# A two-block transformer on one core: the first norm ahead of the state-space set-up, four gate tiles in the state-space stage

## The chip, the cores and the metric
The kernel runs on one core of one Trainium2 chip. The metric is the device time of one execution in microseconds (us). The engines are PE (TensorE, matmul), DVE (VectorE), ACT (ScalarE), POOL (GpSimd) and SP (SyncE, which issues most DMAs). Each engine takes its instructions from one queue, in order.

## The reference, cut to what matters
The change lies in the first quarter of the program, the token mixer. What follows it (a channel mixer, then attention, cross attention and an MLP) is the same in both kernels.

```
h = rmsnorm(x, g_pre)                      # x: 528 tokens x 1024 (16 meta tokens ahead of 512)
u, q, k, v, o, gi, gf, ga, gb = split(h @ w_in)
y_a = gelu(s5_ssm(u, lam, b, c, d, log_dt)) # state space, 32 groups of 16 inputs, 64 states
y_a = y_a * sigmoid(y_a @ w_glu)
hb  = mlstm_chunkwise(conv_silu(q), conv_silu(k), v, gi, gf)   # 4 heads of 128
y_b = rmsnorm_per_head(hb) * sigmoid(o)
merged = sigmoid(ga) * (y_a @ w_a) + sigmoid(gb) * (y_b @ w_b)
x + rmsnorm(merged @ w_out, g_post)
...
def rmsnorm(x, g):
    return x * lax.rsqrt(mean(x * x) + 1e-6) * g
```

## The kernel before
Activations lie as 128 features by tokens. A float32 product is made of three passes of a rounded type: the operands are split into a high and a low part, and PE runs high x high, high x low and low x high. Of a weight tile of 128 output columns, 1024 x 128 numbers come in one DMA (`wst`); ACT rounds them to `whi` (line 125) and DVE, in the mLSTM stage POOL for a part of them, subtracts to get `wlo` (line 126). `product` then gives pieces: for each token range of 264 (or 258 and 256) columns, 24 matmuls in three pieces (lines 165, 167, 168), and an eviction behind the last. Eviction of the w_in products multiplies by `rs`, the reciprocal root of the first norm, so no w_in product can leave its PSUM bank before that norm is known. Banks are of two kinds, `mm` and `mx`, taken in turn.

The norm: `next_input` makes the accumulators `nacc`; `add_square` has ACT square each x tile and adds the squares (the first of each accumulator's chain on POOL, the rest on DVE, line 241). `rstd_wide` sums over the partitions with matmuls by a tile of ones (line 257, bank `rs`), ACT takes Ln and Exp (lines 258, 259), and DVE takes one Newton step in four operations (lines 261 to 264). It runs once for each half of the tokens.

The set-up of the state space (`ssm_setup`) is a generator: powers of the complex decay rates by repeated multiplication on DVE (lines 360 to 365, four products, a difference and a sum each), scaled copies of them (404 to 433), and eight products on POOL (395 to 397). It is written behind the norm. `ssm_tile` computes the state space for one of four feature tiles: a set-up product `pp` (451 to 453), transposing matmuls (`tr`, 461 and 485), DVE rotations and scans (519 to 533, the last of them is `xx`), matmuls on `xx` (539), and a gelu (550 to 553) into `ya`. `weave` lays product pieces between these steps: q, k, v and o of the mLSTM (`raw`, eviction in line 719). In the mLSTM stage the fill is the 16 gate tiles (`gate`, eviction in line 791, tanh in 792), and behind them the products of w_glu, which need `ya` and the ring tiles that the heads' o gates leave.

The order of each engine's queue is not that of the source. The framework is opened with `schedule_with_timeline_sim=True` and sorts the instructions of each engine by a plan of its own; `keep_in_program_order` and `issue_after` bind single instructions. Which instruction stands where is therefore read from the built kernels, how long it takes from the trace.

Of the kernel before, what the change touches and what calls it, by code (L numbers as in the profile page):

```python
# [11 lines left out]
FT = mybir.dt.float32  # L12
FR = mybir.dt.float32r
# [6 lines left out]
P = 128  # L20
# [43 lines left out]
class Net:  # L64
# [184 lines left out]
    def rstd_wide(self, out, accs, t, width=DM):  # L249


        nc = self.nc
        V = nc.vector
        n = out.shape[-1]
        ps = self.pmm.tile([P, 512], FT, name="rs", bufs=1)[:, 0:n]
        for j, acc in enumerate(accs):
            nc.tensor.matmul(ps, self.ones, acc, start=j == 0, stop=j == len(accs) - 1)
        nc.scalar.activation(out, ps, AF.Ln, scale=1.0 / width, bias=self.eps)
        nc.scalar.activation(out, out, AF.Exp, scale=-0.5)
        t = t[:, 0:n]  # L260
        V.tensor_tensor(t, out, out, OP.mult)
        V.scalar_tensor_tensor(t, ps, EPS * width, t, OP.add, OP.mult)
        V.tensor_scalar(t, t, -0.5 / width, 1.5, OP.mult, OP.add)
        V.tensor_tensor(out, out, t, OP.mult)
# [32 lines left out]
    def ssm_setup(self, pool, tmp):  # L297
# [106 lines left out]
        V.tensor_scalar(self.al, pr, pos, None, OP.mult)  # L404
        V.tensor_scalar(self.be, pi, -1.0, None, OP.mult)
        for j in range(TC):
            V.tensor_copy(self.qr[:, j, :], pr[:, TC - 1 - j, :])
            V.tensor_scalar(self.qi[:, j, :], pi[:, TC - 1 - j, :], neg, None, OP.mult)
# [21 lines left out]
        V.tensor_copy(hir[:, 8, :], er[9])  # L430
        V.tensor_copy(hii[:, 8, :], ei[9])
        V.tensor_scalar(loi, loi, pos, None, OP.mult)
        V.tensor_scalar(hii, hii, pos, None, OP.mult)
# [270 lines left out]
    def mixer(self):  # L704
# [3 lines left out]
        with ExitStack() as es:  # L708
# [5 lines left out]
            yas = [self.yab.tile([P, L], FT, name=f"ya{f}") for f in range(4)]  # L714
            raws = {}

            def raw(i, h):
                t = raws[i, h] = self.ring.tile([P, L], FT, name=f"r{4 * h + i}")
                return self.product(I["w_in"][4 + 4 * i + h], FULL, lambda ps, t0, n: V.tensor_tensor(
                    t[:, t0:t0 + n], ps, self.rs[:, t0:t0 + n], OP.mult))  # L720

            with ExitStack() as e2:
# [4 lines left out]
                with tc.tile_pool(name="tmp0", bufs=1, side="right", reuse_waits="tile") as tmp:  # L727
                    self.next_input(extra=tmp, more=1)
# [32 lines left out]
                    for (t0, n) in FULL:  # L761
                        self.rstd_wide(rs[:, t0:t0 + n], [a[:, t0:t0 + n] for a in self.nacc],
                                       tmp.tile([P, 264], FT, name="rw"))
# [3 lines left out]
                    for _ in setup:  # L767
                        pass
                self.ssmp = self.pool(e2, "ssmp", 2)
                self.ssmt = self.pool(e2, "ssmt")  # L770
                load, fill = self.chain([self.gate_rows(mx)] + [raw(i, h) for h in range(4) for i in range(4)])
# [7 lines left out]
                self.weave([(steps, fill[first:])])  # L779
                self.pmx = None  # L780
            sgp = self.pool(es, "sgp")
            mt = self.pool(es, "mtmp", 2)
            sga = [sgp.tile([P, LQ], FT, name=f"sga{f}") for f in range(KT)]
            ybs = [self.yab.tile([P, L], FT, name=f"yb{h}") for h in range(4)]
            gb = {}

            def gate(f, out):

                def ev(ps, t0, n):
                    o = out()[:, t0 - T0:t0 - T0 + n]  # L790
                    V.tensor_tensor(o, ps, rs[:, t0:t0 + n], OP.mult)
                    nc.scalar.activation(o, o, AF.Tanh, scale=0.5)
                return self.product(I["w_in"][f], TAIL, ev)
# [6 lines left out]
            with ExitStack() as e2:  # L800
# [10 lines left out]
                gates = [gate(20 + f, lambda f=f: sga[f]) for f in range(KT)] + [  # L811
# [46 lines left out]
            jobs = self.merge(self.pool(es, "memp"), mt, yas, ybs, sga, gb, sgp, a2, b2)  # L858
# [36 lines left out]
    def merge(self, mem, mt, yas, ybs, sga, gb, sgp, a2, b2):  # L895
# [32 lines left out]
        yo = [sgp.tile([P, LQ], FT, name=f"sga{f}") for f in range(KT)]  # L928
# [154 lines left out]
    def bias_rows(self, mt):  # L1083


        nc = self.nc
        self.ed = self.dram.tile([12, P, 640], FT, name="ed")
        self.gd = self.dram.tile([12, 640], FT, name="gd")
        rel = mt.tile([32, 12], FT, name="rel", bufs=1)
        nc.sync.dma_start(rel, self.I["rel"])  # L1090
        for i in range(2):
            c = slice(320 * i, 320 * i + 320)
            oh, am, g = (self.yab.tile([P, L], FT, name=f"{n}{i + j}")[0:m, 0:320]
                         for n, j, m in (("ya", 0, 32), ("ya", 2, 12), ("yb", 0, 12)))
# [440 lines left out]
    def memory_input(self, mp):  # L1535
# [395 lines left out]
```

## Time and profile before

| | |
|---|---|
| time, median of 3 runs | 1567.07 us (1562.07 to 1567.22) |
| profiled execution: own time | 1567.67 us |
| profiled execution: span, first to last instruction | 1564.4 us |
| mean granted TensorE clock | 0.981 of full speed |
| busy PE, DVE, ACT, POOL | 95%, 66%, 46%, 21% |

The profile is of one execution, 3.3 us of which lie outside its span. Its own time stands 0.6 us above the median, so a sum made against it can be compared with the median as it is. The shares are means over stages of different kinds; the first 350 us, which the change touches, are read on their own below.

### The profile page before, as it was taken

What the parts mean: (1) busy time and instruction counts of PE and PEld (TensorE: products, weight loads), DVE (VectorE), ACT (ScalarE), POOL (GpSimd) and SP (SyncE); (2) the same over time, 40 slices, a digit from 0 to 9 for tenths busy, and PEclk for the clock granted to TensorE, in tenths of its full rate; (3) what the DMA queues carried; (4) which work ended last, traced back from release to release, by engine and by line L of the source; (5) the groups of instructions that cost most, each with busy time, mean ns of one, the idle gap of its engine ahead of it and who ended that gap; (6) DMA issues with size and microseconds to landing.
All of it is one profiled execution on the core that took longest, in us unless ns stands there. A gap on an engine that the chain in (4) does not pass through costs nothing.

```text
span 1564.4 us, 25002 instructions
## 1 busy us (share of the span) xinstructions
PE 1479.6 (95%) x9761; PEld 1334.2 (85%) x9761; DVE 1032.0 (66%) x1968; ACT 724.1 (46%) x1400; POOL 335.5 (21%) x308
## 2 busy tenths in 40 slices
PE   5998999999989999999999999999789999999997
PEld 4988999988989899999999877877778888888886
DVE  8887879777577655555475878888887443344334
ACT  5233356664554433334455466575666431134332
POOL 4066721003342000000131445303342000000001
PEclk9998999999999999999999999999999999999998
DMA  5333232227444322223656222113220322333221
GB/s 189 96 98 105 80 120 75 64 74 234 148 136 135 95 93 93 90 95 118 187 152 217 78 67 68 55 44 125 90 81 32 93 95 93 96 94 96 93 94 54
DMA packets 66430, 161.95 MB, mean 104 GB/s; under 512 B 15100, under 2 KB 24556, under 8 KB 66184
## 3 DMA queue, kind: packets, MB, share of 16 engines
q1 hardware_dynamic: 64936, 157.74, 32.3%
q8 instruction: 76, 1.25, 0.3%
q0 software_dynamic: 288, 1.57, 0.3%
q10 hardware_dynamic: 1088, 1.05, 0.2%
q14 instruction: 42, 0.34, 0.1%
HBM read 153.92 MB, written 10.33 MB: 105 GB/s over the span
## 4 chain that ended last, share of the span: by engine, by line
PE 54%; DVE 10%; ACT 3%; issue 1%; DMA 1%; POOL 0%; DVEq 0%; ACTq 0%; POOLq 0%
PE mm L135 6%; PE mm L138 5%; PE mm L136 5%; PE mm L165 5%; PE mm L168 5%; PE mm L167 5%; PE mx L165 4%; PE mx L168 4%; PE mx L167 4%; DVE xl L110 2%; PE mx L135 2%; PE mx L138 2%; PE mx L136 2%; DVE ptl L107 1%; PE tr L1208 1%
## 5 line engine op out<-in xcount | busy, mean ns | idle before, releaser
L126 DVE TENSOR_TENSOR wlo<-wst,whi 128x1024 fp32r<-128x1024 f32 (+2 forms) x227 | 285.0, 1257 | 196.9 <-ACT whi L125 121.2
L125 ACT ACTIVATE whi<-wst 128x1024 fp32r<-128x1024 f32 (+3 forms) x244 | 251.9, 1034 | 302.9 <-PE mm L136 107.3
L168 PE MATMUL mm<-xl,whi 128*128 128x256 f32 (+4 forms) x808 | 233.5, 314 | 0.3 <-DVE xl L110 0.3
L167 PE MATMUL mm<-xh,whi 128*128 128x256 f32 (+4 forms) x808 | 233.1, 314 | 0.2 <-DVE x L1641 0.2
L167 PE MATMUL mx<-xh,whi 128*128 128x512 f32 (+4 forms) x552 | 170.6, 330 | 7.8 <-ACT xh L109 7.7
L168 PE MATMUL mx<-xl,whi 128*128 128x512 f32 (+4 forms) x552 | 170.9, 330 | 3.3 <-DVE xl L110 3.2
L167 PEld LDWEIGHTS mm<-xh,whi 128*128 128x128 f32 (+1 forms) x808 | 153.8, 190 | 9.9 <-DVE x L1670 0.3
L168 PEld LDWEIGHTS mm<-xl,whi 128*128 128x128 f32 (+1 forms) x808 | 153.3, 190 | 10.3 <-issue 0.6
L165 PE MATMUL mm<-xh,wlo 128*128 128x256 f32 (+4 forms) x808 | 139.2, 311 | 0.0
L135 PE MATMUL mm<-hh,whi 128*128 128x256 f32 (+1 forms) x496 | 139.2, 310 | 0.0
L136 PE MATMUL mm<-hl,whi 128*128 128x256 f32 (+1 forms) x496 | 139.0, 310 | 0.0
L165 PEld LDWEIGHTS mm<-xh,wlo 128*128 128x128 f32 (+1 forms) x808 | 116.4, 187 | 9.8 <-issue 0.5
L167 PEld LDWEIGHTS mx<-xh,whi 128*128 128x128 f32 (+1 forms) x552 | 105.8, 192 | 17.1 <-ACT xh L109 8.0
L168 PEld LDWEIGHTS mx<-xl,whi 128*128 128x128 f32 (+1 forms) x552 | 105.6, 191 | 14.3 <-DVE xl L110 4.9
L165 PE MATMUL mx<-xh,wlo 128*128 128x512 f32 (+4 forms) x552 | 104.6, 331 | 0.0
L126 POOL TENSOR_TENSOR wlo<-wst,whi 128x1024 fp32r<-128x1024 f32 (+1 forms) x34 | 75.2, 2217 | 120.5 <-PE mm L138 38.2
L993 POOL TENSOR_TENSOR acc<-acc,osq 128x256 f32<-128x256 f32 (+1 forms) x26 | 25.2, 969 | 344.6 <-ACT osq L990 344.6
L135 PEld LDWEIGHTS mm<-hh,whi 128*128 128x128 f32 x496 | 93.4, 188 | 6.1
L136 PEld LDWEIGHTS mm<-hl,whi 128*128 128x128 f32 x496 | 93.5, 189 | 5.8
L165 PEld LDWEIGHTS mx<-xh,wlo 128*128 128x128 f32 (+1 forms) x552 | 85.5, 193 | 9.4 <-issue 0.2
L138 PE MATMUL mm<-hh,wlo 128*128 128x256 f32 (+1 forms) x496 | 83.6, 310 | 1.9 <-DVE wlo L126 1.9
L138 PEld LDWEIGHTS mm<-hh,wlo 128*128 128x128 f32 x496 | 70.5, 188 | 8.0 <-DVE wlo L126 2.3
(553 smaller groups left out, 3353.3 us busy)
## 6 DMA issues: line engine op xcount, KB each, us to landing
wst<-in_w_in_dram SPq DMA_DIRECT2D x52, 512.0 KB, 3.6
wst<-in_w_down_dram SPq DMA_DIRECT2D x32, 512.0 KB, 3.5
wst<-in_w_mup_dram SPq DMA_DIRECT2D x32, 512.0 KB, 3.5
wst<-in_w_mdown_dram SPq DMA_DIRECT2D x32, 512.0 KB, 3.7
wst<-in_w_gate_dram SPq DMA_DIRECT2D x22, 512.0 KB, 3.5
wst<-in_w_up_dram SPq DMA_DIRECT2D x22, 512.0 KB, 3.6
wst<-in_w_out_dram SPq DMA_DIRECT2D x20, 512.0 KB, 3.6
wst<-in_w_down_dram SPq DMA_DIRECT2D x16, 384.0 KB, 3.5
```

Of the source, the lines that this page charges most:

```text
L107: nc.vector.tensor_tensor(lo, src, hi.bitcast(FT), OP.subtract)
L110: nc.vector.scalar_tensor_tensor(lo, src, gain, hi.bitcast(FT), OP.mult, OP.subtract)
L125: nc.scalar.activation(hi[:, 0:n], st[:, 0:n], AF.Copy)
L126: self.wlow.tensor_tensor(lo[:, 0:n], st[:, 0:n], hi[:, 0:n].bitcast(FT), OP.subtract)
L135: nc.tensor.matmul(ps, ah, bh, start=start and i == 0, stop=False)
L136: nc.tensor.matmul(ps, ah, bl, start=False, stop=False)
L138: nc.tensor.matmul(ps, al, bh, start=False, stop=stop and i == n - 1)
L165: nc.tensor.matmul(ps, wl[:, k], xh, start=False, stop=k == KT - 1)
L167: nc.tensor.matmul(ps, wh[:, k], xh, start=k == 0, stop=False)
L168: nc.tensor.matmul(ps, wh[:, k], xl, start=False, stop=False)
L993: nc.gpsimd.tensor_tensor(acc, acc, sq, OP.add)
L1208: nc.tensor.matmul(yp[0:64, c0:c1], m[:, j, vc:vc + 64], d[:, j - f0, c0:c1], start=ji == x == 0, stop=ji == len(jobs) - 1 and x == 2)
```

## The change
The first norm uses four accumulators in place of two, so that POOL adds two squares and not six, and four ones-matmuls for each half of the tokens and not two. Its banks come from the pool `ptr` and its small tile is one for each half. The rest of the set-up is issued behind the norm's last DVE operation. Twenty scaled copies of the set-up go from DVE to ACT. Four of the sixteen gate tiles (w_in 20 to 23) become fill of the state-space stage, whose list of steps gets eight more empty ones; their output tiles and the mLSTM's `yb` tiles get pools of their own.

```diff
-    def rstd_wide(self, out, accs, t, width=DM):
+    def rstd_wide(self, out, accs, t, width=DM, bank=None):
-        ps = self.pmm.tile([P, 512], FT, name="rs", bufs=1)[:, 0:n]
+        ps = (self.pmm.tile([P, 512], FT, name="rs", bufs=1) if bank is None else bank)[:, 0:n]
         for j, acc in enumerate(accs):
-            nc.tensor.matmul(ps, self.ones, acc, start=j == 0, stop=j == len(accs) - 1)
+            mm = nc.tensor.matmul(ps, self.ones, acc, start=j == 0, stop=j == len(accs) - 1)
+            if bank is not None and j == 0:
+                self.tc.keep_in_program_order(mm)
...
-        V.tensor_tensor(out, out, t, OP.mult)
+        return V.tensor_tensor(out, out, t, OP.mult)
...
-        V.tensor_scalar(self.al, pr, pos, None, OP.mult)
-        V.tensor_scalar(self.be, pi, -1.0, None, OP.mult)
+        copy = lambda to, t, scale=1.0: nc.scalar.activation(to, t, AF.Copy, scale=scale)
+        copy(self.al, pr, pos)
+        copy(self.be, pi, -1.0)
         for j in range(TC):
-            V.tensor_copy(self.qr[:, j, :], pr[:, TC - 1 - j, :])
-            V.tensor_scalar(self.qi[:, j, :], pi[:, TC - 1 - j, :], neg, None, OP.mult)
+            copy(self.qr[:, j, :], pr[:, TC - 1 - j, :])
+            copy(self.qi[:, j, :], pi[:, TC - 1 - j, :], neg)
...
+            sgs = [self.pool(es, "sgp")] * 4
+            sga = [sgs[0].tile([P, LQ], FT, name=f"sga{f}") for f in range(4)]
...
-                    self.next_input(extra=tmp, more=1)
+                    self.next_input(extra=tmp, more=3)
...
-                        self.rstd_wide(rs[:, t0:t0 + n], [a[:, t0:t0 + n] for a in self.nacc],
-                                       tmp.tile([P, 264], FT, name="rw"))
+                        known = self.rstd_wide(rs[:, t0:t0 + n], [a[:, t0:t0 + n] for a in self.nacc],
+                                               tmp.tile([P, 264], FT, name=f"rw{t0}"),
+                                               bank=self.ptr.tile([P, 512], FT, name="tr"))
...
-                    for _ in setup:
-                        pass
+                    with tc.issue_after(known.ins):
+                        for _ in setup:
+                            pass
...
-                load, fill = self.chain([self.gate_rows(mx)] + [raw(i, h) for h in range(4) for i in range(4)])
+                load, fill = self.chain([self.gate_rows(mx)] + [raw(i, h) for h in range(4) for i in range(4)] + [
+                    gate(20 + f, lambda f=f: sga[f]) for f in range(4)])
...
-                self.weave([(steps, fill[first:])])
+                self.weave([(steps + [None] * 8, fill[first:])])
...
-                gates = [gate(20 + f, lambda f=f: sga[f]) for f in range(KT)] + [
+                gates = [gate(20 + f, lambda f=f: sga[f]) for f in range(4, KT)] + [
                     gate(28 + f, lambda f=f: gate_b(f)) for f in range(KT)]
```

From the start of the merge on, the order of every engine's instructions is the same in both kernels. Three places ahead of it:

DVE at the norm. Before, the four steps of the first half (rw, rw, rw, rs) stand among set-up operations (al, be, qi, cm, sm):

```order
L261 TENSOR_TENSOR rw<-rs 128x264
L405 TENSOR_SCALAR be<-pi 128x288
L408 TENSOR_SCALAR qi<-pi,sg 128x32 x3
L360 TENSOR_TENSOR cm_523<-sm_181 128x32
L262 SCALAR_TENSOR_TENSOR rw<-rs,rw 128x264
L361 TENSOR_TENSOR cm_524<-sm_180 128x32
L263 TENSOR_SCALAR rw<-rw 128x264
L362 TENSOR_TENSOR sm_599<-cm_523,cm_524 128x32
L264 TENSOR_TENSOR rs<-rs,rw 128x264
```

In the changed kernel the two halves stand together, and the first set-up operation behind them is the memset of `zero`:

```order
L263 TENSOR_TENSOR rw_359<-rs 128x264
L264 SCALAR_TENSOR_TENSOR rw_359<-tr,rw_359 128x264
L265 TENSOR_SCALAR rw_359<-rw_359 128x264
L266 TENSOR_TENSOR rs<-rs,rw_359 128x264
L263 TENSOR_TENSOR rw_371<-rs 128x264
L751 TENSOR_TENSOR u<-mx,rs 128x33x8 x2
L264 SCALAR_TENSOR_TENSOR rw_371<-tr,rw_371 128x264
L126 TENSOR_TENSOR wlo<-wst,whi 128x64
L265 TENSOR_SCALAR rw_371<-rw_371 128x264
L266 TENSOR_TENSOR rs<-rs,rw_371 128x264
L346 MEMSET zero 16x128
```

The set-up's decay powers are all behind the norm now, and the first evictions of u (line 738 before, 751 now) stand between the norm's halves.

DVE in state-space tile 1, around the `xx` of its first half. Before, the gelu of tile 0, its steps on u and ya (lines 550, 551, 553), stands ahead of it:

```order
L550 TENSOR_SCALAR u<-u 128x528
L466 TENSOR_TENSOR ks<-ks,dd 16x4x16
L551 TENSOR_TENSOR u<-u,yv 128x528
L719 TENSOR_TENSOR r_741<-mx,rs 128x264
L530 TENSOR_TENSOR r<-r,ec 128x264
L531 TENSOR_TENSOR rs<-rs,es 128x264
L553 SCALAR_TENSOR_TENSOR ya_106<-u,yv 128x8x66
L533 TENSOR_TENSOR xx<-r,rs 128x4x65
```

In the changed kernel (lines 553, 554, 556, and 536 for `xx`) they stand behind it:

```order
L536 TENSOR_TENSOR xx<-r,rs 128x4x65
L553 TENSOR_SCALAR u<-u 128x528
L724 TENSOR_TENSOR r_746<-mx,rs 128x264
L554 TENSOR_TENSOR u<-u,yv 128x528
L556 SCALAR_TENSOR_TENSOR ya_106<-u,yv 128x8x66
L469 TENSOR_TENSOR ks<-ks,dd 16x4x16
```

The matmul that waits for `xx` has three DVE operations fewer ahead of it.

PE in the mLSTM stage, second half of head 2 (`st` scores, `num` and `den` their products with v and with ones). Before, products of gate tiles (L167, L168, into mm) stand between:

```order
L168 MATMUL mm<-xl_133,whi 128x258
L135 MATMUL st<-qh,kh 128x256
L136 MATMUL st<-ql,kh 128x256
L138 MATMUL st<-qh,kl 128x256
L167 MATMUL mm<-xh_126,whi 128x258
L168 MATMUL mm<-xl_134,whi 128x258
L135 MATMUL st<-qh,kh 128x128
L136 MATMUL st<-ql,kh 128x128
L138 MATMUL st<-qh,kl 128x128
```

In the changed kernel the gates are used up at this place:

```order
L138 MATMUL num<-sh,vl 128x256
L686 MATMUL den<-sl,ones_85 2x256
L135 MATMUL st<-qh,kh 128x256
L136 MATMUL st<-ql,kh 128x256
L138 MATMUL st<-qh,kl 128x256
L135 MATMUL st<-qh,kh 128x128
L136 MATMUL st<-ql,kh 128x128
L138 MATMUL st<-qh,kl 128x128
L135 MATMUL num<-sh,vh 128x256
L685 MATMUL den<-sh,ones_85 2x256
```

For 40 rows there is nothing between the head's own matmuls. w_glu's products come behind them.

## Rows read from the trace of the kernel before

**Rows 1.** The page, part 1: engine, busy us, share of the span, instructions.
```profile
PE 1479.6 (95%) x9761; PEld 1334.2 (85%) x9761; DVE 1032.0 (66%) x1968; ACT 724.1 (46%) x1400; POOL 335.5 (21%) x308
```

**Rows 2.** Waits of PE from 0 to 400 us: total, times, longest.
```profile
PE rs L257 <- DVE cm L361: 8.9, 1, 8.9
...
PE tr L539 <- DVE xx L533: 5.9, 3, 4.0
PE tr L461 <- DVE pp L453: 2.7, 1, 2.7
...
PE tr L601 <- DVE r L588: 1.1, 1, 1.1
PE st L695 <- ACT sqn L689: 1.0, 1, 1.0
```

**Rows 3.** PE by time around the norm: start, us, engine, line, operation, tiles, idle before.
```profile
27.19 0.71 PE L257 MATMUL rs<-nacc,ones 128*128 128x264 f32 x2 [1.72 <-DVE nacc L241]
...
37.92 2.10 PE L257 MATMUL rs<-nacc,ones 128*128 128x264 f32 x4 [8.93 <-DVE cm L361]
39.48 0.75 PE L167 MATMUL mx<-xh,whi 128*128 128x264 f32 x1
```

**Rows 4.** ACT by time, from the last square to the root.
```profile
27.17 0.42 ACT L240 ACTIVATE sq<-x 128x264 f32<-128x264 f32 x1 [3.24 <-DVE nacc L241]
27.61 1.28 ACT L199 ACT_TABLE_LOAD   x1
...
29.42 0.42 ACT L259 ACTIVATE rs<-rs 128x264 f32<-128x264 f32 x1
```

**Rows 5.** DVE by time, set-up and norm beside each other.
```profile
27.33 0.23 DVE L389 TENSOR_SCALAR sm<-sm,sg 128x32 f32<-128x32 f32 x1
...
30.70 1.38 DVE L408 TENSOR_SCALAR qi<-pi,sg 128x32 f32<-128x32 f32 x2
...
35.41 0.42 DVE L261 TENSOR_TENSOR rw<-rs 128x264 f32<-128x264 f32 x1
...
38.69 1.12 DVE L738 TENSOR_TENSOR u<-mx,rs 128x264 f32<-128x264 f32 x2
```

**Rows 6.** POOL by time: one of the eight set-up products.
```profile
33.27 1.32 POOL L397 TENSOR_TENSOR bb<-bb,tb 128x512 f32<-128x512 f32 x1
```

**Rows 7.** Stretches: length, busy PE, PEld, DVE, ACT, POOL, granted clock (PEclk), DMA.
```profile
36.00:44.00 8.00, 6.08 (x35) 5.42 (x36) 7.11 (x30) 0.91 (x2) 1.00 (x1) 0.69 0.02 6
38.60:90.70 52.10, 48.36 (x383) 45.82 (x381) 45.46 (x143) 13.46 (x16) 8.27 (x7) 0.98 0.35 93
92.00:96.00 4.00, 4.00 (x21) 3.90 (x20) 2.37 (x5) 0.46 (x1) 2.04 (x2) 0.57 0.64 204
148.00:160.00 12.00, 12.00 (x68) 12.00 (x68) 5.59 (x14) 3.67 (x7) 6.65 (x6) 0.63 0.32 92
180.00:188.00 8.00, 8.00 (x44) 8.00 (x43) 5.17 (x12) 1.84 (x5) 5.88 (x7) 0.57 0.44 113
212.00:340.00 128.00, 128.00 (x1026) 117.75 (x1025) 104.47 (x220) 79.34 (x174) 12.69 (x19) 1.00 0.25 80
```

**Rows 8.** DVE by time, the end of the last set-up product.
```profile
89.91 0.75 DVE L453 TENSOR_TENSOR pp<-pp,tp 128x576 f32<-128x576 f32 x1
```

**Rows 9.** DVE by time, ahead of the longest wait of the state space.
```profile
142.11 0.40 DVE L550 TENSOR_SCALAR u<-u 128x528 f32<-128x528 f32 x1
...
142.57 0.69 DVE L551 TENSOR_TENSOR u<-u,yv 128x528 f32<-128x528 f32 x1
...
144.22 1.82 DVE L553 SCALAR_TENSOR_TENSOR ya<-u,yv 128x528 f32<-128x528 f32 x1
145.88 1.07 DVE L533 TENSOR_TENSOR xx<-r,rs 128x260 f32<-128x260 f32 x1
```

**Rows 10.** DVE groups by shape, 300 to 340 us: count, busy us, mean ns.
```profile
L107 DVE TENSOR_TENSOR sl<-dt,sh 128x256 fp32r<-128x256 f32 x6 | 2.8, 472 | 1.5 <-ACT sh L106 1.5
L672 DVE TENSOR_TENSOR dt<-st,dt 128x256 f32<-128x256 f32 x6 | 2.5, 415 | 1.0 <-PE st L138 1.0
```

More of the change, by code (lines that the diff above doesn't have):

```diff
@@ L429, in ssm_setup @@
                 cmul(tr[:, n:2 * n, :], ti[:, n:2 * n, :], tr[:, 0:n, :], ti[:, 0:n, :], er[at], ei[at], n)
[L430 to L433, printed above, removed]
+        copy(hir[:, 8, :], er[9])
+        copy(hii[:, 8, :], ei[9])
+        copy(loi, loi, pos)
+        copy(hii, hii, pos)
         self.rot = (lor, loi, hir, hii)
@@ L720, in raw, with gate, ev @@
                     t[:, t0:t0 + n], ps, self.rs[:, t0:t0 + n], OP.mult))
+            def gate(f, out):
+                def ev(ps, t0, n):
+                    o = out()[:, t0 - T0:t0 - T0 + n]
+                    V.tensor_tensor(o, ps, self.rs[:, t0:t0 + n], OP.mult)
+                    nc.scalar.activation(o, o, AF.Tanh, scale=0.5)
+                return self.product(I["w_in"][f], TAIL, ev)
             with ExitStack() as e2:
@@ L778, in mixer @@
                     steps += [self.ssm_tile(ft, uds[ft], yas[ft])] + [None] * 8
-                self.weave([(steps, fill[first:])])
+                self.weave([(steps + [None] * 8, fill[first:])])
                 self.pmx = None
-            sgp = self.pool(es, "sgp")
+            sgp = self.pool(es, "sgp2")
+            sgs += [sgp] * 4
+            sga += [sgp.tile([P, LQ], FT, name=f"sga{f}") for f in range(4, KT)]
             mt = self.pool(es, "mtmp", 2)
-            sga = [sgp.tile([P, LQ], FT, name=f"sga{f}") for f in range(KT)]
-            ybs = [self.yab.tile([P, L], FT, name=f"yb{h}") for h in range(4)]
+            self.ybp = self.pool(es, "ybp")
+            ybs = [self.ybp.tile([P, L], FT, name=f"yb{h}") for h in range(4)]
             gb = {}
[L787 to L793, printed above, removed]
             def gate_b(f):
@@ L857, in mixer @@
             self.pmx = self.pool(es, "pmx2", 3, PS)
-            jobs = self.merge(self.pool(es, "memp"), mt, yas, ybs, sga, gb, sgp, a2, b2)
+            jobs = self.merge(self.pool(es, "memp"), mt, yas, ybs, sga, gb, sgs, a2, b2)
         self.ffn(*jobs)
@@ L893, in glu_jobs, with merge @@
                      for i in range(2)]
-    def merge(self, mem, mt, yas, ybs, sga, gb, sgp, a2, b2):
+    def merge(self, mem, mt, yas, ybs, sga, gb, sgs, a2, b2):
         nc = self.nc
@@ L927, in merge @@
         self.next_input()
-        yo = [sgp.tile([P, LQ], FT, name=f"sga{f}") for f in range(KT)]
+        yo = [sgs[f].tile([P, LQ], FT, name=f"sga{f}") for f in range(KT)]
         memory = self.memory_input(mem)
@@ L1092, in bias_rows @@
             c = slice(320 * i, 320 * i + 320)
-            oh, am, g = (self.yab.tile([P, L], FT, name=f"{n}{i + j}")[0:m, 0:320]
+            oh, am, g = ((self.yab if n == "ya" else self.ybp).tile([P, L], FT, name=f"{n}{i + j}")[0:m, 0:320]
                          for n, j, m in (("ya", 0, 32), ("ya", 2, 12), ("yb", 0, 12)))
@@ L1545, in memory_input @@
             if k % 2 == 0:
-                pair = [self.yab.tile([P, L], FR, name=f"{n}{k // 2}") for n in ("ya", "yb")]
+                pair = [p.tile([P, L], FR, name=f"{n}{k // 2}") for n, p in (("ya", self.yab), ("yb", self.ybp))]
             for m, t in zip((mh, ml), pair):
```

## Prediction

> **What bounds the kernel now.** I read the page first. PE is busy 95% of the span [rows 1], so the kernel can gain little but PE's idle time and the time that PE runs at a low clock. All engines' orders agree from the merge on, some 350 us into the run, so only what lies ahead of it counts. There the waits of PE [rows 2] name five places that the change can touch: the bank of the norm's second half (8.9 us), `xx` in the state space (5.9 us in three waits, one of 4.0), the set-up product `pp` (2.7), the gate rows' transposes (1.1) and one sum in the mLSTM (1.0). Third, the stretches [rows 7]: after an idle time PE's granted clock falls from full speed (2.4 GHz) towards half (1.2), and 8, 12 or 8 us at a mean of 0.69, 0.63 or 0.57 go by. From 212 to 340 us PE is never idle and the clock is full: there nothing is to be had, only lost.
>
> **The norm.** By the time lines the last square waits 3.24 us for an accumulator and ends at 27.59; then come a table load of 1.28, Ln and Exp, which ends at 29.84 [rows 4]. DVE takes the root up at 35.41 only, because set-up operations are ahead in its queue, and the first eviction of u starts at 38.69 [rows 5]. PE ran out of banks at 29.0 (8.93 ahead of 37.92) and has its next product at 39.48 [rows 3]. In the change the squares go into four accumulators and POOL adds two, so I take the 3.24 away: last square done at 24.4, roots at 26.6, then DVE without set-up in between. Its four steps cost about 0.4 each (L261 is 0.42), 1.6 in all, so the first eviction starts at about 28.2 and ends at 28.8. PE has its own work until then: 29.0 as before, less the 1.72 of idle time at 27.19, plus four more ones-matmuls of 0.71 each [rows 3], that is 30.1 at most. I let products go on at 29.3 (the bounds are 28.8 and 30.1): **10.2 us** won. The clock is also saved: 36 to 44 at 0.69 loses 0.31 x 8 = 2.5 us [rows 7], of which half of the 3.48 up to 39.48, 1.7, is in the 10.2 already; 0.7 is left.
>
> **The set-up, and its price for the first state-space matmul.** It now starts about 28.8. Between the norm and the last `pp` DVE was 45.5 us busy in 52.1 [rows 7]; `pp` ended at 90.66 [rows 8]. In the changed order 42 more rows lie in that stretch (183 for 141). Some 33 small ones at 0.2 (a lone one took 0.23 [rows 5]) and nine larger ones come to about 7.5; one more weight subtraction and a few evictions, 1.3; the norm's second half and the scaled copies that leave take 2.7 away: 51.6. The copies lie on ACT, 13.5 busy of 52.1 there [rows 7]: twenty at less than the 0.42 of a square of 264 columns [rows 4], under 8.4 in all, spread over 50 us: I cost them at nothing, and at 8.4 as the end if PE waited for each.
>
> POOL's eight products of about 1.3 each [rows 6] now meet this DVE work. Two set-up operations on DVE took 1.38 beside POOL, where a like one took 0.23 alone [rows 5]; some five such operations stand in 27 to 38 us, 4 to 5 us together. I add 3, because some of that pattern repeats whatever I do; the bounds are 0 and 8 x 1.3 = 10.4. The Trainium skill says in "SBUF — State Buffer", "Who interferes with whom", that a DVE operation which needs the pair of ports that DVE and GpSimd share is fully blocked while the other holds it. The stretched rows agree with it. By that rule each of the eight products would cost DVE its whole length, and the time would be that of the first rival, 1558, in place of 1550.
>
> So DVE is ready at 28.2 + 51.6 + 3, about 82.8. PE reached that matmul at 90.80 - 2.71 = 88.1 [rows 2]; it comes 10.9 earlier from the norm, 0.6 from the gate rows' wait, and has 77 more matmuls of product ahead by the order, at 0.12 each (128 us for 1026 matmuls from 212 us on [rows 7]) 9.2: about 85.8. So `pp` should be in time by 3 us. I leave 1.5 of the 3.8 us of both waits: **2.3 us** won. The stretch behind (92 to 96 at 0.57) lost 4 x 0.43 = **1.7**, all saved.
>
> **State space.** Ahead of the 4.0 us wait stand three gelu steps, 0.40 + 0.69 + 1.82 = 2.9 us, of which 2.6 directly hold up `xx` [rows 9]. They are behind it now, so this wait becomes about 2.0 (not 1.4, because DVE is fuller, see above). The two others share 1.9 [rows 2]; DVE has less ahead of the later one, too, and I put the three at 3.0 in place of 5.9: **2.9**. The clock behind them lost 12 x 0.37 + 8 x 0.43 = 7.9 [rows 7]; I leave 3: **4.9**.
>
> **Four gate tiles.** By the count of products ahead of the first mLSTM scores, the kernel before had done 5.8 gate tiles there and the changed one 7.4: its own order had pulled gates forward already. So 1.6 tiles really move, 1.6 x 48 x 0.12 = 9.2 us of PE, the same 9.2 as ahead of the first state-space matmul. As PE work it is neutral. Their weights come sooner, and no wait for a DMA stands in [rows 2]; the pools of their own for `yb` and the gates only place memory. Both cost nothing, unless a tile waits for the one that lay there before, which would stand at the first gate eviction. But the mLSTM now uses its gates up early: in the second half of head 2 there are 40 rows without any fill, 5.0 us of PE at about 0.125. w_glu's products can't fill them, they need the ring tile of head 2's o gate, which this half frees. DVE has 21 operations in the same stretch, scores, parts, maxima, evictions; at 0.41 to 0.47 the larger ones [rows 10], some 8.4 us. PE waits for the difference, 3.4, and then runs slower for a while, which I put at 2: 4.4 were lost at 148 to 160 [rows 7] after a wait of 4.0 [rows 2], and this wait is likely split. **-5.4 us**, bounds 0 (DVE works ahead) and 10 (each unit's chain in full).
>
> **Sum**: 10.2 + 0.7 + 2.3 + 1.7 + 2.9 + 4.9 - 5.4 = 17.3. From the profiled execution's 1567.67 that is **1550.4 us**. That execution and the median are 0.6 us apart, so I give the same number for the median, 1550.
>
> **Rivals.**
> 1. *The set-up comes too late.* If every POOL product blocks DVE for its length (10.4 and not 3), `pp` is ready at 90.2, 4.4 after PE, half clock behind it costs 2 more, and `xx` in the first tiles comes as late: the 2.3 + 1.7 are gone, and about half of the 7.8 in the state space with them. 17.3 - 7.9 = 9.4 won: 1558. For it: DVE's stretched rows. Against it: the same rows show only five stretched operations beside eight products.
> 2. *The hole in head 2 is larger*: 8 us and 4 of clock in place of 5.4: 10.7 won, 1557. For it: no row of fill in the order. Against it: PE waited just once, 1.0 us, at this kind of sum [rows 2].
> 3. *The holes all close.* No loss in head 2, and none of the 3 + 3 + 1.5 that I left: 17.3 + 5.4 + 7.5 = 30.2, 1537.5; most of it gives 1538 to 1544.
> 4. *The planner gives it back.* DVE, and not PE, sets the pace from the norm to the end of the state space; what PE wins at the norm it waits for again before `pp` and `xx`. DVE is 87% busy from 38.6 to 90.7 [rows 7], so this would need the idle 6.6 us to remain as it was, and the gain is 0 to 6 us: 1562 to 1568. This is also the case in which the change doesn't do what it says, since gates had been pulled forward before.
> 5. *Slower.* The last two heads without fill run at the length of their dependencies: 0.47 and 0.415 for two of a unit's DVE steps [rows 10] and some 1.5 for its other four (mask, exp, scores, rounding, at sizes like these), 2.4 in all, times nine units is 21.6, where I have 3.4, and 5 for the clock. It decides above 22.7 us of loss there. It comes to 26.6: 1571.5. Against it: the units overlap in the trace, and the order has 63, 49 and 12 rows of fill behind the empty stretch.
>
> **How the numbers follow.** The forecast (1544 to 1556) gets 0.50, rival 1 0.16, rival 2 0.13, rival 3 0.09, rival 4 0.07, rival 5 0.05. The range 1541 to 1562 leaves out half of rival 3 and rivals 4 and 5, under 2 in 10. Within 0.5% is 7.8 us, 1559.2 to 1574.9, about what a measurement of this kernel can tell from no change. Faster: the forecast, rival 3, and about two thirds of rivals 1 and 2: 0.78. Same: the rest of these, rival 4 and nearly all of rival 5: 0.18. Slower: 0.04.
>
> **What would show it.** Norm: PE without the 8.9 us wait and its products going on near 29 us; wrong if a wait for `rs` or the u eviction stands there. Set-up: the wait at L464 (461 before) under 1.5 us, PE there at about 85; wrong if it is above 3. State space: the wait for `xx` behind the gelu at 2 us and no stretch under 0.6 of clock after 148 us. Head 2: one hole of 3 to 4 us in front of its second sum, then clock below full speed. The forecast fails as a whole if the state-space stage ends less than 15 us earlier than before or if head 2 and 3 together idle more than 12 us.

## The result and the profile after

Four runs of the changed kernel have a median of 1551.41 us (1548.21 to 1555.60), beside 1566.24 us for the kernel before; the ratio is 0.9914, 95% interval 0.9893 to 0.9936. A second set of runs (below, `after_again`) gave 0.9903 (0.9884 to 0.9922). The gain is 13 to 15 us, for 17 forecast. The profiled execution took 1552.2 us.

The head of the page of the changed kernel, with busy time by engine:

```profile
span 1550.5 us, 25022 instructions
...
PE 1474.9 (95%) x9769; PEld 1326.8 (86%) x9769; DVE 1027.4 (66%) x1946; ACT 728.2 (47%) x1420; POOL 329.9 (21%) x304
```

Against [rows 1] PE is 4.7 us less busy and the span 13.9 us shorter. The waits of PE from 0 to 400 us, in the changed kernel (line 464 is 461 before, 542 is 539, 604 is 601, 698 is 695, 858 is 847; the waits of the start and those inside the merge are left out):

```profile
PE tr L542 <- DVE xx L536: 3.9, 5, 1.5
PE tr L464 <- ACT ks L467: 2.6, 2, 1.5
...
PE mm L167 <- DVE u L751: 2.3, 1, 2.3
PE st L858 <- ACT rows L854: 1.7, 1, 1.7
PE tr L604 <- DVE r L591: 1.4, 1, 1.4
PE st L698 <- ACT sqn L692: 1.4, 1, 1.4
...
PE tr L464 <- DVE pp L456: 0.6, 1, 0.6
```

The 8.9 us wait of [rows 2] is gone, and of those shown none is as long; the longest single one is 2.3. But there are more of them: the eviction of u (line 751) and the kernel scale `ks` (line 467) are new. PE by time at the norm shows the first and what the norm gave:

```profile
25.17 2.39 PE L257 MATMUL tr<-nacc,ones 128*128 128x264 f32 x10
...
30.07 0.29 PE L167 MATMUL mx<-xh,whi 128*128 128x264 f32 x1
...
44.26 0.29 PE L167 MATMUL mm<-xh,whi 128*8 128x264 f32 x1 [2.34 <-DVE u L751]
```

The products behind the norm go on at 30.07, where [rows 3] have 39.48: 9.4 us earlier. Ahead of both stand the same matmuls but for the four ones-matmuls more. At 44.26 PE has stood 2.34 us for the eviction of a bank. DVE by time tells what it stood for:

```profile
26.78 0.43 DVE L263 TENSOR_TENSOR rw<-rs 128x264 f32<-128x264 f32 x1 [0.43 <-ACT rs L261]
...
28.91 1.13 DVE L751 TENSOR_TENSOR u<-mx,rs 128x264 f32<-128x264 f32 x2
...
39.87 0.66 DVE L751 TENSOR_TENSOR u<-mx,rs 128x264 f32<-128x264 f32 x1 [2.83 <-DMA ud<-u]
...
41.15 1.03 DVE L362 TENSOR_TENSOR cm<-pr 128x128 f32<-128x128 f32 x1
42.10 0.28 DVE L363 TENSOR_TENSOR cm<-pi 128x128 f32<-128x128 f32 x1
...
43.58 0.63 DVE L751 TENSOR_TENSOR u<-mm,rs 128x264 f32<-128x264 f32 x1
...
45.65 1.36 DVE L365 TENSOR_TENSOR cm<-pr,pi 128x128 f32<-128x128 f32 x1
```

The root's steps stand alone now (26.78, where [rows 5] have 35.41), and u is evicted at 28.91. But at 37.04 DVE has nothing it may do: the next eviction writes a u buffer whose store to memory has not landed, and 2.83 us pass. Behind it come the operations beside POOL's set-up products, 1.03 and 1.36 us long; an operation of the same shape that began just before POOL's next product took 0.28 (line 363, at 42.10). The eviction that PE waits for starts at 43.58. Stretches of the changed kernel (columns as in [rows 7]):

```profile
28.20:91.50 63.30, 59.18 (x469) 55.89 (x467) 58.23 (x193) 19.54 (x38) 16.41 (x14) 0.97 0.42 112
44.00:48.00 4.00, 3.74 (x20) 2.34 (x21) 4.00 (x4) 1.53 (x5) 3.90 (x3) 0.62 0.47 90
92.00:212.00 120.00, 113.07 (x921) 107.91 (x920) 100.49 (x165) 47.83 (x87) 81.80 (x65) 1.00 0.35 100
212.00:300.00 88.00, 88.00 (x716) 82.14 (x715) 76.27 (x155) 56.32 (x121) 12.08 (x13) 1.00 0.30 91
300.00:320.00 20.00, 18.08 (x134) 14.45 (x133) 15.50 (x40) 11.32 (x32) 2.01 (x5) 1.00 0.10 30
307.20:316.50 9.30, 7.38 (x49) 4.81 (x48) 7.44 (x21) 4.31 (x12) 1.55 (x4) 1.00 0.19 57
```

From the norm to the first `pp` DVE is busy 58.2 of 63.3 us. The clock falls behind the 2.34 us wait (0.62 from 44 to 48), but from 92 to 212 us it is full, where before the two stretches behind the `xx` waits had 0.63 and 0.57 [rows 7]. From 300 to 320 PE is idle 1.9 us, all of it in the stretch of head 2 without fill (307.2 to 316.5), and the clock stays full.

The matmuls on `xx`, the last ones of the state space on PE, before and in the changed kernel, with their first and last start:

```profile
L539 PE MATMUL tr<-xx,pp x64: 218/275/478, 115.8 to 215.3; 128*128 128x66 f32 x64
```

```profile
L542 PE MATMUL tr<-xx,pp x64: 219/275/325, 115.4 to 209.6; 128*128 128x66 f32 x64
```

The state space ends 5.7 us earlier on PE. But 73 product matmuls more than before (1344 for 1271) are done ahead of the mLSTM's first scores.

To place the time, I summed over stretches of 4 us what PE stood idle, and what the clock cost (busy PE times one less the granted clock), from the first product matmul to the first matmul of the merge; behind that matmul all the kernels have the same number of matmuls to run, in an order that differs in a few rows. All figures are of one profiled execution each.

| kernel | first product to merge, us | of it idle | lost by clock | the rest: work | behind the merge |
|---|---|---|---|---|---|
| before | 347.0 | 22.6 | 11.2 | 313.2 | 1209.3 |
| changed | 334.7 | 16.0 | 1.6 | 317.1 | 1208.6 |

Of 12.3 us, 6.6 come from idle time and 9.6 from the clock, and 3.9 go to work. The norm's two waits alone (8.9 and 1.7) gave 10.6 us of idle time, and the other places together took 4.0 of it back. The four ones-matmuls more are eight rows at 0.2 us from start to start, 1.6 us; most of the rest of the 3.9 is that the clock's column counts too much. `unbound` (below) runs the same number of matmuls as the changed kernel and has 3.6 us less work by this sum, with 13.7 more lost by the clock. So the clock's 9.6 are nearer 7. The remaining 1.6 of the 13.9 are an earlier start (0.9) and 0.7 behind the merge.

### The profile page after: what moved, and what is told of

It is laid out like the page before. It is cut to its first block, busy times and chain, and to the rows that moved or that the text cites. A ratio compares the mean times of both kernels' runs of the same rounds, so it can differ in the third digit from the quotient of the medians.

```text
span 1550.5 us, 25022 instructions
## 1 busy us (share of the span) xinstructions
PE 1474.9 (95%) x9769; PEld 1326.8 (86%) x9769; DVE 1027.4 (66%) x1946; ACT 728.2 (47%) x1420; POOL 329.9 (21%) x304
## 4 chain that ended last, share of the span: by engine, by line
PE 55%; DVE 10%; ACT 3%; issue 1%; POOL 0%; ACTq 0%; DVEq 0%; POOLq 0%
PE mm L135 6%; PE mm L138 6%; PE mm L136 6%; PE mm L165 5%; PE mm L168 5%; PE mm L167 5%; PE mx L165 4%; PE mx L168 4%; PE mx L167 4%; DVE xl L110 2%; PE mx L135 2%; PE mx L138 2%; PE mx L136 2%; DVE ptl L107 1%; PE tr L1219 1%
## 5 line engine op out<-in xcount | busy, mean ns | idle before, releaser
L167 PE MATMUL mm<-xh,whi 128*128 128x256 f32 (+4 forms) x792 | 228.7, 314 | 2.5 <-DVE u L751 2.3
L168 PE MATMUL mm<-xl,whi 128*128 128x256 f32 (+4 forms) x792 | 229.3, 314 | 0.3 <-DVE xl L110 0.3
L167 PE MATMUL mx<-xh,whi 128*128 128x512 f32 (+3 forms) x584 | 176.5, 324 | 7.5 <-ACT xh L109 6.8
L168 PE MATMUL mx<-xl,whi 128*128 128x512 f32 (+3 forms) x584 | 177.6, 326 | 3.3 <-DVE xl L110 3.2
L167 PEld LDWEIGHTS mm<-xh,whi 128*128 128x128 f32 (+1 forms) x792 | 149.8, 189 | 12.9 <-DVE u L751 2.6
L168 PEld LDWEIGHTS mm<-xl,whi 128*128 128x128 f32 (+1 forms) x792 | 149.7, 189 | 10.6 <-issue 0.6
L167 PEld LDWEIGHTS mx<-xh,whi 128*128 128x128 f32 x584 | 110.5, 189 | 16.7 <-ACT xh L109 7.1
L168 PEld LDWEIGHTS mx<-xl,whi 128*128 128x128 f32 x584 | 110.3, 189 | 14.3 <-DVE xl L110 5.0
L165 PE MATMUL mx<-xh,wlo 128*128 128x512 f32 (+3 forms) x584 | 105.9, 322 | 0.0
L165 PEld LDWEIGHTS mx<-xh,wlo 128*128 128x128 f32 x584 | 87.1, 187 | 9.1
```

Of the source, the lines that this page charges most:

```text
L165: nc.tensor.matmul(ps, wl[:, k], xh, start=False, stop=k == KT - 1)
L167: nc.tensor.matmul(ps, wh[:, k], xh, start=k == 0, stop=False)
L168: nc.tensor.matmul(ps, wh[:, k], xl, start=False, stop=False)
```

## The experiments

All are edits of the changed kernel, except where said. Ratios are to the kernel before, on the same chip; 0.0010 is 1.6 us. "To the merge" is the time of the table above. The planner sorts the queues anew for each edit. By the traces only `half_bb` keeps the changed kernel's order of PE, DVE and ACT row for row, and `gates_kept` keeps it up to 178 us; the other edits change the order in other places too, so that what they show is the edit and the new order together.

**All gates in the mLSTM (`gates_kept`).**

```diff
-    [raw(i, h) for h in range(4) for i in range(4)] + [gate(20 + f, lambda f=f: sga[f]) for f in range(4)])
+    [raw(i, h) for h in range(4) for i in range(4)])
...
-    self.weave([(steps + [None] * 8, fill[first:])])
+    self.weave([(steps, fill[first:])])
...
-    gates = [gate(20 + f, lambda f=f: sga[f]) for f in range(4, KT)] + [
+    gates = [gate(20 + f, lambda f=f: sga[f]) for f in range(KT)] + [
```

> The changed kernel, but all sixteen gate tiles stay fill of the mLSTM stage. Theory A (the gain is the norm's and the clock's; moving gates only moves PE work): the hole of 1.9 us in head 2 goes, and the time is 1549 to 1553 us. Theory B (the moved gates fill waits in the state space): waits for xx there grow, the clock falls behind one of them, and the time is 1555 to 1560.

Measured: 1549.5 us, 0.9903 (0.9887 to 0.9919). Theory A's time. But its reason was wrong. The waits of PE from 300 to 345 us, where the hole in head 2 was to go:

```profile
PE st L698 <- ACT sqn L692: 1.6, 1, 1.6
PE st L135 <- DVE dt L675: 0.2, 1, 0.2
```

The hole is as large as before the edit (1.8 us, and 1.9 in the changed kernel). The orders say why: with or without the four gates in the source's state-space list, 1344 matmuls of w_in products stand ahead of the first scores of the mLSTM (1271 before), and the stretch of head 2 without fill is as long, 49 and 47 rows in the two traces. The planner draws the gates forward by itself. From 178 us on the two orders differ in places. Clock by stretch:

```profile
184.00:188.00 4.00, 2.80 (x24) 2.59 (x23) 3.36 (x8) 2.21 (x4) 1.85 (x3) 1.00 0.61 179
188.00:192.00 4.00, 3.70 (x19) 3.70 (x20) 2.15 (x4) 1.29 (x3) 3.84 (x4) 0.60 0.18 38
192.00:196.00 4.00, 4.00 (x22) 4.00 (x22) 0.77 (x2) 0.77 (x2) 1.50 (x2) 0.55 0.48 176
```

Behind a wait of 1.50 us for `xx`, ended at 188.30, the clock falls to about half here. To the merge this execution took 340.5 us, the changed kernel's first 334.7.

**The gates alone (`gates_only`)**: the changed kernel with the norm, the tie and the copies taken back.

```diff
-    self.next_input(extra=tmp, more=3)
+    self.next_input(extra=tmp, more=1)
...
-    bank=self.ptr.tile([P, 512], FT, name="tr"))
...
-    with tc.issue_after(known.ins):
-        for _ in setup:
-            pass
+    for _ in setup:
+        pass
...
-    copy(self.al, pr, pos)
+    V.tensor_scalar(self.al, pr, pos, None, OP.mult)
...
```

> The kernel before with the four gate tiles moved and nothing else (two accumulators, bank rs, set-up not held behind the norm, copies on DVE). Theory A: the 8.9 us wait for the norm's bank is there as before, and the time is within 3 us of before, 1563 to 1569. Theory B: 1556 to 1562, with the half-clock stretches of the state space gone though the norm's wait is still there.

Measured: 1566.75 us, 1.0018 (1.0007 to 1.0029), slower by 2.8 us, in theory A's range. The 8.9 us wait stood as in [rows 2], and the half-clock stretches too (some 11.5 us lost to the merge). In this kernel the move does change the order: 1340 product matmuls stand ahead of the first scores, 1271 before, and head 2 has a hole of 2.5 us.

**The norm alone (`norm_only`)**: `gates_kept` with the copies on DVE as in the next experiment.

> The kernel before with the norm's part alone: four accumulators, banks from the other pool, the set-up held behind the norm; copies on DVE and all gates in the mLSTM as before. Theory A (nearly all of the gain is the norm's, and the copies are worth some 4 us beside it): 1552 to 1556 us. Theory B (the parts work only together): 1558 to 1564.

Measured: 1555.32 us, 0.9950 (0.9933 to 0.9967). Theory A's time: 7.8 us of the gain come without gates and copies. The planner puts 1372 product matmuls ahead of the first scores here, more than with the gates moved, and head 2 has a hole of 2.8 us.

**The copies on DVE (`copies_dve`, `copies_dve_again`).**

```diff
-    copy(self.al, pr, pos)
-    copy(self.be, pi, -1.0)
+    V.tensor_scalar(self.al, pr, pos, None, OP.mult)
+    V.tensor_scalar(self.be, pi, -1.0, None, OP.mult)
...
-        copy(self.qr[:, j, :], pr[:, TC - 1 - j, :])
-        copy(self.qi[:, j, :], pi[:, TC - 1 - j, :], neg)
+        V.tensor_copy(self.qr[:, j, :], pr[:, TC - 1 - j, :])
+        V.tensor_scalar(self.qi[:, j, :], pi[:, TC - 1 - j, :], neg, None, OP.mult)
```

> The changed kernel with the twenty scaled copies of the set-up on DVE again. Theory A (DVE sets when pp is ready, it had only 0.6 us of wait of PE left there): the copies cost DVE 4 to 8 us beside POOL, pp comes 3 to 6 us later, PE waits for it and runs at half clock behind it: 1555 to 1559 us. Theory B (DVE has slack there): within 2 us of the changed kernel, 1550 to 1553.

> The kernel with the scaled copies on DVE once more, on the same chip as the changed kernel. Theory A (the copies are worth what they take from DVE ahead of pp, about 4 us): slower than the changed kernel by 3 to 5 us. Theory B (the first comparison, 4.5 us by the ratios, was the spread of the executions): within 2 us of it.

Measured: 1556.01 us, 0.9943 (0.9925 to 0.9961), and 1552.86 us, 0.9921 (0.9903 to 0.9940). The two are 4.5 and 2.8 us above the changed kernel's two ratios, and the intervals overlap both times. Beside `gates_kept` and `u4`, which ran on the first one's chip and have the copies on ACT, the first is slower, clear of the intervals (0.9925 at the least for it, 0.9919 at the most for them). So the copies are worth some 3 to 6 us. The last set-up product's line, first start and last, in the changed kernel and with the copies on DVE:

```profile
L456 DVE TENSOR_TENSOR pp<-pp,tp x8: 742/756/1460, 90.2 to 166.9; 128x576 f32<-128x576 f32 x8
```

```profile
L456 DVE TENSOR_TENSOR pp<-pp,tp x8: 741/758/1454, 96.2 to 172.6; 128x576 f32<-128x576 f32 x8
```

`pp` is 6.0 us later (in the second pair 5.7). That is not all a cost: the order has 38 product matmuls more ahead of it, 4.6 us at 0.12 each, and PE waits only 0.9 us for `pp`, in the changed kernel 0.6. What PE waits for is the kernel scale; its waits from 130 to 215 us:

```profile
PE tr L464 <- ACT ks L467: 3.2, 2, 2.5
```

The changed kernel has 2.6 in two waits of 1.5 at most. Behind the 2.5 us wait the clock falls, and the copies' two profiles lose 3.0 and 3.3 us by it in the state space, the changed kernel's two nothing. To the merge it is 338.8 and 343.1 us, where the changed kernel has 334.7 and 337.4; the idle time is 17.1 and 17.4 us, there 16.0 and 17.6. Theory A's time the first time, short of its range by a little the second; its reason, that PE stands at `pp`, is not shown.

**Four buffers for u (`u4`, `gates_kept_u4`).**

```diff
-    u = tmp.tile([P, TC, NC], FT, name="u", bufs=2)
+    u = tmp.tile([P, TC, NC], FT, name="u", bufs=4)
```

> The changed kernel with four buffers for u in place of two, so that no eviction of u waits for the store of an earlier one. Theory A (the new 2.3 us wait of PE near 44 us is that store: DVE stood 2.8 us before the third tile's eviction): the wait and the slow clock behind it are gone, DVE is 2 to 3 us earlier at pp too, and the time is 1546 to 1549 us. Theory B (the wait comes from DVE operations stretched beside POOL's products): PE still waits over 1.5 us at 44, and the time is 1550 to 1552.

> All gates in the mLSTM as before and four buffers for u, the rest as changed. Theory A (DVE sets the pace up to pp, so a wait taken away at 44 us comes back at the gate rows' transposes): the same as with the gates kept, within 1.5 us, and the wait at the transposes is 3 us. Theory B (the two edits add up): 2 to 4 us faster than the changed kernel.

Measured: 1549.32 us, 0.9903 (0.9886 to 0.9919), and 1549.63 us, 0.9905 (0.9886 to 0.9924). Cause right, gain not: the wait at 44 us is gone, so it does not come about without the store (`half_bb`, below, shows that it needs POOL as well). In its place, PE's waits from 20 to 92 us in `u4`:

```profile
PE tr L604 <- DVE r L591: 3.4, 1, 3.4
```

It was 1.4, and 3.0 in the changed kernel's second profile. `pp` starts at 91.0, as before the edit (90.2 and 90.8). What DVE gets back from the store it does not turn into an earlier `pp`, and PE, which comes sooner, waits at the next place. With all gates kept PE waits 2.9 us there, and `pp` starts at 88.9, 1.7 us sooner than in `gates_kept`. Neither is shown to be faster than the changed kernel.

**Less work on POOL (`half_bb`)**, which leaves out four of the six products of lines 397 to 399.

```diff
-    nc.gpsimd.tensor_tensor(tb, bc[:, b], wide(z), OP.mult)
-    nc.gpsimd.tensor_tensor(bb[:, a], bb[:, a], tb, OP.add)
```

> The changed kernel without four of the six products on POOL in the set-up (the second term of the input matrix is left out: tb and its addition). Theory A (DVE sets the pace from the norm to the first state-space matmul, and operations stretched beside POOL are a part of that): the stretched DVE operations between 40 and 48 us are gone, some 4 us of DVE time, the wait of 2.3 us at 44 us shrinks under 1, pp is ready 3 to 4 us earlier, and the time falls by 2 to 4 us, 1547 to 1549. Theory B (POOL is no part of it, the store of u alone makes the wait): the wait near 44 us stays at 2 or more and the time stays within 1.5 us of 1551.

Measured: 1553.1 us, 0.9940 (0.9918 to 0.9961). DVE by time:

```profile
39.22 0.65 DVE L749 TENSOR_TENSOR u<-mx,rs 128x264 f32<-128x264 f32 x1 [2.29 <-DMA ud<-u]
...
40.50 0.29 DVE L362 TENSOR_TENSOR cm<-pr 128x128 f32<-128x128 f32 x1
...
41.59 0.63 DVE L749 TENSOR_TENSOR u<-mm,rs 128x264 f32<-128x264 f32 x1
```

The store's wait stays at 2.29 us, but the operation that took 1.03 takes 0.29, and the eviction comes at 41.59 in place of 43.58; PE waits 0.5 us there. `pp` is ready 3.5 us earlier (86.7 to 90.2):

```profile
L454 DVE TENSOR_TENSOR pp<-pp,tp x8: 743/755/1461, 86.7 to 163.4; 128x576 f32<-128x576 f32 x8
```

So POOL costs DVE what theory A said. The time did not follow: to the merge it took 334.8 us, as the changed kernel did, with 2.7 us less idle and 3.4 more lost by the clock, nearly all in the state space. By the ratio it is even 4 to 6 us above the changed kernel, though the intervals overlap; the profiled execution is the shortest of its four, so this has no profile and stays open. Theory A is right on the mechanism, wrong on its worth.

**Without the tie (`unbound`).**

```diff
-    with tc.issue_after(known.ins):
-        for _ in setup:
-            pass
+    for _ in setup:
+        pass
```

> The changed kernel without the tie that holds the set-up behind the norm. Theory A (set-up operations among the norm's steps on DVE are what held the norm's bank): the planner puts them there again, PE waits 4 to 9 us for that bank, and the time is 1555 to 1560 us. Theory B (the four accumulators and the banks of the other pool are enough): PE waits under 2 us there, 1549 to 1553.

Measured: 1559.6 us, 0.9972 (0.9958 to 0.9986). PE and DVE by time:

```profile
36.59 0.56 PE L167 MATMUL mx<-xh,whi 128*128 128x264 f32 x1 [6.30 <-DVE u L751]
```

```profile
32.61 1.18 DVE L366 TENSOR_TENSOR cm<-pi,pr 128x128 f32<-128x128 f32 x1
33.71 0.42 DVE L263 TENSOR_TENSOR rw<-rs 128x264 f32<-128x264 f32 x1
...
35.81 1.11 DVE L751 TENSOR_TENSOR u<-mx,rs 128x264 f32<-128x264 f32 x2
```

Theory A: set-up operations, stretched beside POOL, are ahead of the root's first step again (33.71 where the changed kernel has 26.78), and PE waits 6.3 us for the first u eviction. Without the tie 9 to 11 us of the gain are lost (0.9972 beside 0.9914 and 0.9903). Theory A had PE wait for the norm's bank; it waits one step on, for the first eviction that uses the norm.

**Two accumulators (`two_acc`).**

```diff
-    self.next_input(extra=tmp, more=3)
+    self.next_input(extra=tmp, more=1)
```

> The changed kernel with two accumulators in the first norm in place of four: POOL adds six squares again, and there are two ones-matmuls for each half. Theory A (the squares' wait of 3.24 us for an accumulator is on the norm's path): the products behind the norm go on 2.5 to 3.5 us later than 30.07, less 1.4 for the ones-matmuls; PE waits about 3 us for the bank or the u eviction, with slow clock behind it; 1553 to 1556 us. Theory B (DVE sets the pace behind it anyway): within 1.5 us of the changed kernel.

Measured: 1559.8 us, 0.9975 (0.9960 to 0.9991), beyond theory A's range, and 11 us above the changed kernel by the ratios measured together. PE by time:

```profile
31.11 0.36 PE L167 MATMUL mx<-xh,whi 128*128 128x264 f32 x1 [2.82 <-DVE u L751]
...
47.44 0.29 PE L167 MATMUL mm<-xh,whi 128*8 128x264 f32 x1 [2.88 <-DVE u L751]
```

The wait of 2.8 us is the one expected, and there is a second of 2.9 in place of 2.3 at the u eviction. To the merge the profiled execution is only 4.6 us later than the changed kernel's on that chip (342.0 to 337.4); it was a short one of its twelve runs (median 1559.8), so the rest of the 11 us has no profile here and stays open.

**The gate rows behind three heads (`rows_later`).**

```diff
-    self.chain([self.gate_rows(mx)] + [raw(i, h) for h in range(4) for i in range(4)] + [
+    self.chain([raw(i, h) for h in range(3) for i in range(4)] + [self.gate_rows(mx)] + [
+        raw(i, 3) for i in range(4)] + [
```

> The changed kernel with the gate rows (a small product, two scans and some ten more operations on DVE, five transposes on PE) behind the products of the first three heads in the fill, so that none of it lies ahead of the first state-space matmul. Theory A (DVE sets the pace from the norm to that matmul): DVE has 7 us less ahead of pp, the wait of 1.4 us at the transposes is gone and pp comes without a wait; 1546 to 1549 us. Theory B (the work is the same and DVE in the state space gets what it loses here): waits for xx grow by 2 us or more and the time is 1550 to 1554.

Measured: 1550.14 us, 0.9922 (0.9905 to 0.9940), theory B's time. Waits of PE from 20 to 212 us:

```profile
PE tr L542 <- DVE xx L536: 5.8, 4, 3.8
PE mm L167 <- DVE u L751: 2.2, 1, 2.2
PE tr L464 <- DVE pp L456: 1.5, 1, 1.5
```

`pp` starts at 84.7, 5.5 us earlier, and the wait at the transposes is gone; `xx` takes 5.8 us in place of 3.9. The work that DVE was spared ahead of `pp` meets it in the state space.

**The changed kernel again (`after_again`).**

> The changed kernel once more, unchanged, with a profile of its own. Theory A (whether TensorE's clock falls behind a given short wait differs from execution to execution): the waits stand where they stood, within 0.5 us each, the idle time up to the merge is again 15 to 17 us, but the clock's loss up to there is another than 1.6 us, 4 to 8 as in the experiments, and the program behind the merge differs from the first profile by 2 us or more. Theory B (the low loss of 1.6 us belongs to this order): it is under 3 again. Ratio to before 0.990 to 0.993 by both.

Measured: 1550.03 us, 0.9903. Waits of PE from 20 to 92 us, and stretches:

```profile
PE tr L604 <- DVE r L591: 3.0, 1, 3.0
PE mm L167 <- DVE u L751: 1.4, 1, 1.4
```

```profile
44.00:48.00 4.00, 4.00 (x35) 3.40 (x34) 3.93 (x6) 1.03 (x2) 3.17 (x2) 1.00 0.61 137
...
60.00:64.00 4.00, 2.28 (x13) 2.29 (x14) 4.00 (x9) 0.00 (x0) 0.00 (x0) 0.79 0.40 128
64.00:68.00 4.00, 4.00 (x29) 4.00 (x28) 3.90 (x18) 0.64 (x1) 0.00 (x0) 0.78 0.24 28
```

The same program has 1.4 and 3.0 us where the first profile had 2.3 and 1.4; so waits differ by up to 1.6 us from execution to execution, more than theory A allowed. Behind the hole in head 2, of 1.9 us again, the clock is 0.79 and 0.78 from 316 to 324 us, where it was full the first time. Idle to the merge is 17.6 us and the clock's loss 3.0, just the bound between the theories. `half_bb`, whose PE runs the same matmuls in the same order, lost 5.0; so the low loss of the first profile is not shown to be this order's. Behind the merge it took 1203.6 us, 5.0 less than in the first profile.

## Why the prediction was right, point by point

The time came out as forecast, 1551.4 for 1550, and the two largest gains, the norm and the clock in the state space, were there. The nearness is in part luck: the set-up and the waits of the state space gave some 8 us less than forecast, and the clock of the state space and the gates in head 2 cost some 6 less.

- **The norm**, forecast 10.2 us (products on at 29.3, at most 30.1): 9.4, at 30.07. The cause is shown: with the set-up among the root's steps again (`unbound`) PE waits 6.3 us there. The clock behind it, 0.7, was saved.
- **The set-up**, forecast 2.3 us: the two waits named fell from 3.8 to 2.0, but the eviction of u took 2.3 that the prediction did not have, so the stage's waits grew by 0.5 us. The failed step is "DVE is ready at 28.2 + 51.6 + 3, about 82.8". It was ready at 91.5. DVE was busy 58.2 us, 3.6 more than counted, and idle 5.1. A part of the 3.6 is the sum itself: 33 operations at 0.2 are 6.6 us of its 7.5, which leaves 0.1 each for the nine called larger, and an operation of 128x128 took 0.28. The idle time should have been read off the kernel before: in 38.6 to 90.7 its DVE was idle 6.6 us [rows 7], and I dropped all of it, though a store that must land does not get quicker. PE came 5.3 us late too (91.1 for 85.8), so `pp` was waited for only 0.6 us. The first rival had `pp` at 90.2, by POOL alone (10.4 us). Four products cost 3.5 us (`half_bb`); beside the three others the profile has operations of 1.08, 1.07 and 1.19 us too, where ones of those shapes take 0.2 to 0.3. From these rows I estimate POOL's whole part at some 6 us, twice the 3 assumed; idle time is most of the rest. "SBUF — State Buffer" of the Trainium skill, "Who interferes with whom", has one side blocked while the other holds the shared ports; the trace agrees where operations meet (1.03 for 0.28), but not every product met one. The prediction spoke of eight such products: the source has six, and the `qt` of the first tile.
- **The clock behind `pp`** (1.7) was saved, and 1.5 lost behind the wait at 44 us in the first profile, 1.4 behind that at 62 us in the second.
- **State space**, forecast 2.9 of idle time and 4.9 of clock. The gelu behind `xx` did shorten the 4.0 us wait: none is above 1.5. But idle time from 92 to 212 us is 6.9 for 6.1 before: `xx` has 3.9 for 5.9, and `ks`, on ACT, 2.6 for 0.3. So the 2.9 us of idle time did not come. The whole gain there is the clock: 7.9 were lost behind the two waits before, nothing in the changed kernel's two profiles, and some 3 in most of the experiments with the norm changed in full, where the forecast left 3. In these profiles, cutting a long wait into short ones was worth more than the time waited. Which of the short ones the clock falls behind is not settled (below).
- **Four gate tiles**, forecast -5.4 us: the hole in head 2 is 1.9 us, and the wait of the merge's first transposes grew by 1.3, with the old 1.0 gone: -2.2, with no clock lost in the first profile; in the second 1.7 was lost there, near the 2 forecast. The 8.4 us of DVE work was laid against 5.0 of PE. In the trace PE is busy 7.4 of the stretch's 9.3 us, and DVE 7.4: scores of the next unit run between (units overlap). And the step that names the gates as cause is wrong: `gates_kept` has as many products ahead of the scores and the same hole. Moving them does nothing in this kernel; alone (`gates_only`) it costs 2.8 us.
- **What the parts are worth**: norm 7.8 us by itself; the copies 3 to 7 on top (2.8 and 4.5 beside the changed kernel, 6.2 beside `gates_kept`, 7.3 between `norm_only` and `gates_kept`, which ran on different chips); gates none. The copies I had only as a part of 2.7 us of DVE time. How they come to be worth more is not settled: the profiles show it in the clock behind one wait for `ks`, and to the merge `norm_only` (339.7 us) is no longer than `gates_kept` (340.5). The norm's own two means need each other: without the tie or without the four accumulators, some 9 to 11 us are lost.
- **The rivals.** Rival 4, that DVE sets the pace up to `pp`, is right as a mechanism: take away the store's wait (`u4`), POOL's products (`half_bb`) or the gate rows (`rows_later`), and `pp` or PE comes sooner, but PE waits at the next place or the clock falls. It did not take back the norm's gain: `pp` came no sooner than before (91.5 for 90.7), but by then PE had run 73 products more (the forecast had 77; 8.8 us at its price of 0.12), which the stages behind no longer had to. Rivals 2 and 5 fell: the hole is 1.9 us and not 8 or more.
- **The signs of being wrong.** One of the two for the forecast as a whole was met although the time came out: the state space ends only 5.7 us earlier, where 15 were asked. The sign left out the products that move ahead of that end. The forecast's own terms up to there, 22.7 us less 9.2 for these products, come to 13.5, so that it would have failed with every term right. With the 8.8 us of the 73 products the measured gain there is 14.5 us.

No experiment is shown to be faster than the changed kernel.

## What to carry to other kernels

Where a reduction's result frees every buffer of the engine that bounds, tie the other work of its engine behind it, and count that work's idle time along with its busy time when the cover moves. On an engine that was 92% busy here, one wait taken away came back, in part or whole, at the next consumer. Small copies moved to an idle engine paid; POOL's products taken away from beside it did not, so such an edit has to be measured by its time and not by the wait that it removes. Before moving pieces in the source for a planner that sorts them, compare the built orders: here it had moved them already.

## What was not expected of the hardware

The granted clock does not follow a wait's length alone. Before, it was 0.57 from 180 to 188 us [rows 7], behind a wait of 1.53 us; in the changed kernel a wait of 1.50 us at 187.89 left it at 1.00, and in `gates_kept` one of 1.50 us at 188.30 was followed by 0.60 and 0.55. Behind 2.34 us it was 0.62 for 4 us, behind 3.0 us 0.78, behind 1.4 us full. What decides it, no run here shows.

Behind the merge, where all kernels run the same number of matmuls, profiled executions took 1200.6 to 1209.3 us, with some 48 to 55 us idle and some 4 to 14 us lost by the clock. A run's time goes with its mean clock: of the changed kernel's first four, 0.993 gave 1548.2 us, 0.989 gave 1550.6 and 1552.2, 0.986 gave 1555.6. Differences under some 5 us between two single executions say nothing about a kernel here. Nor is the time to the merge much surer: two executions of one program differed there by 2.7 us (changed) and 4.3 us (copies on DVE), nearly all by the clock in the second pair, while their idle times agreed within 1.6 and 0.3 us. The idle time is the column to compare.
